# Summing weight blocks in the on-chip raw buffer instead of in HBM, in a hybrid conv and attention decoder

## The chip, the cores and the metric

The kernel runs on one core of a Trainium2 chip. The time is device microseconds of one execution of the whole program, the median of the runs that are shown. Beside it stands one execution recorded by the hardware profiler; its span goes from the first to the last instruction.

## The reference

The program is a decoder trunk of two layers on 512 tokens of width 1024, in float32. Layer 0 has a gated short convolution, layer 1 a sliding-window attention with sinks; each is followed by a SwiGLU feed-forward block of inner width 2816. Cut to what matters here:

```python
def swiglu(h, w_gate_up, w_down):
    g, u = jnp.split(h @ w_gate_up, 2, axis=-1)
    return (jax.nn.silu(g) * u) @ w_down

for l in range(DEPTH):                       # DEPTH = 2
    mix = short_conv_mixer(...) if l < N_A else sliding_window_sink_attention(...) @ b_w_o[j]
    h = h + rmsnorm(mix, ...)
    ff = swiglu(rmsnorm(h, ffn_pre_norm[l]), ffn_w_gate_up[l], ffn_w_down[l])
    h = h + rmsnorm(ff, ffn_post_norm[l])
```

## The kernel before, in words

**Products.** Every float32 matrix is split into a high and a low part of the fp32r type, and a product is three matmuls (hi by lo, hi by hi, lo by hi; `mm3`) or, in the gate stage, a wide matmul of the high weights with both parts of the tokens (L1088) and a narrow one of the low weights (L1091). The weights are split on the way: ScalarE copies a raw tile of 128x1024 into the high part (`whi`, L485), VectorE subtracts that from the raw tile for the low part (`wlo`, L486).

**Seven products for eight.** The gate and up columns are worked off in pairs, q = 0 to 9 in each layer (the names have the layer first: g05 is pair 5 of layer 0). A pair is a 2x2 scheme of blocks with seven products, numbered 1 to 7 and run in the order 1, 2, 6, 5, 7, 3, 4 (`gate_jobs`). Each needs a weight block or a sum of blocks. The sums s1 = a + b and s3 = a + c feed products 5 and 7. A third and a fourth sum feed products 6 and 3. For the pairs in `ADDED` (1, 2, 3, 4, 5, 7) these two are made on VectorE from tiles that are there anyway (`Job.add`, L473): product 6 reads a11 + s1 and product 3 reads a12 + (a11 + s1). For the other pairs they are made in HBM too. The down projection of a round (`down_jobs`) goes the same way with four sums in HBM.

**Sums in HBM.** `Sums` holds HBM tiles (`hsum`) and steps: copies of a block into them, then transfers that add another block, all issued on GpSimd's queue by `issue` (L554). The table `BEGIN` says at which stage each group of sums begins; `sum_on(stage)` issues what is left over, starts the new group, and takes one step of each open group. In the gate and down rounds `issue` is called after each job, for one transfer and a sixth of the backlog, each held back until ScalarE's `whi` of the job three ahead is made.

**The line of jobs.** `in_line` runs a layer's gate and down jobs, 106 of them, on TensorE in order. Three jobs ahead of the running one (`LINE_LEAD`), `prepare(j)` splits job j's weights; then it fetches by SP's queue (`Raw.fetch`, L456) each further raw tile whose buffer has been read for the last time, out of a ring of seven (`N_RAW`); then it makes the VectorE add for job j + 1. Raw tiles are fetched in the order of their first use. The pairs and rounds alternate: pairs 0 and 1, pair 2, down round 0, pair 3, pair 4, down round 1, pair 5, pair 6, down round 2, pair 7, pair 8, pair 9, down round 3. So the fetches for pairs 3, 5 and 7 are issued during a down round, those for pair 1 during pair 0.

**Evacuation.** VectorE and ScalarE take a product's PSUM banks into SBUF (L1043, L1066, L655) right behind it, in the same program order as the splits. The order of instructions on TensorE, VectorE, ScalarE and GpSimd is the order in which the code is written.

Of the kernel before, what the change touches and what calls it, by code (L numbers as in the profile page):

```python
# [13 lines left out]
ALU = mybir.AluOpType  # L14
# [4 lines left out]
S = 512  # L19
# [5 lines left out]
PLAIN = 2  # L25

ADDED = (1, 2, 3, 4, 5, 7)

BEGIN = {
# [52 lines left out]
def yoco_kernel(  # L82
# [22 lines left out]
    nc = tc.nc  # L105
# [15 lines left out]
    def name(s):  # L121
        uid[0] += 1
        return f"{s}_{uid[0]}"

    def slot(s, dt=F32, w=S):
        return big.tile([P, w], dt, tag="slot", name=name(s), padded_shape=[P, S])
# [37 lines left out]
    def fetch(src, n=D):  # L164
        raw = wraw.tile([P, D], F32, tag="raw", name=name("raw"))
        dst = raw[:, :n]
        if len(src.shape) == 3:
            src, dst = src.rearrange("k p c -> p k c"), dst.rearrange("p (k c) -> p k c", c=S)
        nc.sync.dma_start(dst, src)
        return raw  # L170

    class Two:


        def __init__(self, s, dt):
            self.of = [slot(s, dt) for _ in range(2)]
# [5 lines left out]
    def split_weights(src, raw=None, slots=False, eng=nc.vector):  # L182
        if raw is None:
            raw = fetch(src)
        if slots:
            hi, lo = Two("whi", F32R), Two("wlo", F32R)
            for h in range(2):
                c = slice(h * S, (h + 1) * S)
                nc.scalar.activation(hi[:, c], raw[:, c], AF.Copy)
                eng.tensor_tensor(out=lo[:, c], in0=raw[:, c], in1=hi[:, c].bitcast(F32),  # L190
                                  op=ALU.subtract)
            return hi, lo
        hi = wsp.tile([P, D], F32R, tag="whi", name=name("whi"))
        lo = wsp.tile([P, D], F32R, tag="wlo", name=name("wlo"))
        nc.scalar.activation(hi, raw, AF.Copy)
        nc.vector.tensor_tensor(out=lo, in0=raw, in1=hi.bitcast(F32), op=ALU.subtract)
        return hi, lo
# [45 lines left out]
    nc.sync.dma_start(xt[6], xT[6])  # L243
    nc.sync.dma_start(xt[7], xT[7])
    later = [fetch(w_in[1, t]) for t in range(min(3, N_RAW - 3))]


# [159 lines left out]
    class Ahead:  # L407
# [6 lines left out]
        def fetch(self, n):  # L414
            for _ in range(n):
                if self.srcs:
                    self.raws.append(fetch(self.srcs.pop(0)))
# [23 lines left out]
    class Raw:  # L441


        def __init__(self, *srcs):
            self.srcs = srcs
            self.widths = [s.shape[0] * S if len(s.shape) == 3 else D for s in srcs]
            self.n = sum(self.widths)

        def fetch(self):
            self.tile, c = wraw.tile([P, D], F32, tag="raw", name=name("raw")), 0  # L450
            for src, n in zip(self.srcs, self.widths):
                dst = self.tile[:, c : c + n]
                if len(src.shape) == 3:
                    src, dst = (src.rearrange("k p c -> p k c"),
                                dst.rearrange("p (k c) -> p k c", c=S))
                nc.sync.dma_start(dst, src)  # L456
                c += n

    class Job:

# [29 lines left out]
    def in_line(jobs, late, paced=True):  # L490

        raws = []
        for j, job in enumerate(jobs):
            for raw in job.raws:
                if raw not in raws:
                    raws.append(raw)
                raw.last = j
        n = [0]

        def prepare(j):  # L500

            if 0 <= j < len(jobs):
                jobs[j].prepare()
            while n[0] < len(raws) and (n[0] < N_RAW or raws[n[0] - N_RAW].last <= j):
                raws[n[0]].fetch()
                n[0] += 1
            if j + 1 < len(jobs):
                jobs[j + 1].add()

        for j in range(-1, LINE_LEAD):  # L510
            prepare(j)
        late = late()
        for j, job in enumerate(jobs):
            if job.run:
                job.run(job)
            prepare(j + LINE_LEAD)
            if paced and j + LINE_LEAD < len(jobs):
                issue(1 + len(issues) // 6, jobs[j + LINE_LEAD].begun)
            for _ in range(1 if paced else max(len(late) - 1, 1)):
                if late and not job.alone:  # L520
                    late.pop(0)()
            late += job.then() or [] if job.then else []
# [22 lines left out]
    def issue(n, behind=None):  # L545

        for dst, src, op in issues[:n]:
            if len(dst.shape) == 3:
                dst, src = (t.rearrange("k (a b) c -> (k a) (b c)", b=4) for t in (dst, src))
            else:  # L550
                dst, src = (t.rearrange("(a b) c -> a (b c)", b=2) for t in (dst, src))
            kw = {} if op is None else {"accum_op": op}
            made = tc.keep_in_program_order(
                nc.gpsimd.dma_start(dst, src, max_dma_last_dim=4 * 4 * S, **kw))  # L554
            if behind is not None:
                tc.add_manual_dep(
                    made.ins, behind.ins.name, mybir.DependencyInfo(
                        mybir.DependencyClass.Sync, mybir.DependencyReason.DATA),
                    reason="pace")
        del issues[:n]  # L560
# [3 lines left out]
    for l in range(2):  # L564
        for q in range((NF - PLAIN) // 2):
            sums_of[f"g{l}{q}"] = Sums([w_gb[l, q, b] for b in (2, 3, 0, 1)], [P, D],
                                        q not in ADDED)
        for rd, (f0, f1) in enumerate(ROUNDS[:-1]):
# [5 lines left out]
    def sum_on(at):  # L574

        issue(len(issues))
        if at in BEGIN:
            summing.append(sums_of[BEGIN[at]])
        for x in summing:
            x.step()  # L580
        summing[:] = [x for x in summing if x.steps]
# [88 lines left out]
    sums = small.tile([P, 4], F32, tag="sums", name=name("sums"))  # L670
# [6 lines left out]
    with tc.manual_schedule(engines=ALL):  # L677
# [25 lines left out]
        for k in range(KT):  # L703
# [7 lines left out]
            for i in range(3):  # L711
                for t in range(3):
                    n = 3 * k + t
# [117 lines left out]
    with tc.manual_schedule(engines=ALL):  # L831
        project(begun[1][2], ws[2], xs)

        def late():
            parts = []
            for f in range(2):
                first, second, taps, third, end = conv(f)
                first(begun[f][0])
                second(begun[f][1])
                parts += [taps, lambda third=third, f=f: third(begun[f][2])]  # L840
                sum_on(f"c{f}")
                issue(len(issues))
            return parts + end()
# [13 lines left out]
        for n in range(4):  # L857
            line[f"w{n}"] = closing = Job([Raw(w_out[n // 2, n % 2])], None)
            closing.slots = True
        in_line([line[n] for n in CONV.split()], late, False)  # L860
        ws = [line[f"w{n}"].w for n in range(4)]

# [109 lines left out]
    def first_weights(l):  # L972
        return ([w_gu[l, f, j] for f in range(2) for j in range(2)]
                + [w_gb[l, 0, b] for b in range(2)])

    sum_on("o0")
    issue(len(issues))
    ahead = Ahead(first_weights(0))
# [9 lines left out]
    def ffn(l, before, ahead, gain, gpres, following):  # L988
# [20 lines left out]
        def gate_jobs(q, factors, out, to, then):  # L1009
# [3 lines left out]
            sums = sums_of[f"g{l}{q}"]  # L1013
            a21, a22, a11, a12 = (Raw(b) for b in sums.blocks)
            s1, s3, *rest = (Raw(b) for b in sums.sums)
            raws = {1: [a11], 2: [a12], 5: [s1], 7: [s3], 4: [a22]}
            if rest:
                raws[6], raws[3] = ([r] for r in rest)
# [134 lines left out]
        with tc.manual_schedule(engines=ALL):  # L1153
# [30 lines left out]
            for rd, (f0, f1) in enumerate(ROUNDS):  # L1184
                last = rd == len(ROUNDS) - 1
                for f in range(max(f0, PLAIN), f1, 2):
                    q = (f - PLAIN) // 2
                    jobs += gate_jobs(q, factors, pair_acts if last else pair_sums, acts[rd],
                                      lambda q=q: sum_on(f"{l}p{q}"))
                    if behind_one and not (last and f < f1 - 2):  # L1190
                        jobs += behind_one.pop()
                if last:
                    break
                down = down_jobs(range(f0 // 2, f1 // 2), acts[rd], rd == 0,
                                 sums_of[f"d{l}{rd}"],
                                 lambda rd=rd: sum_on(f"{l}s{rd}"))
                behind_one.append(down)
            n = f1 - f0
# [6 lines left out]
            for at, job in zip(LAST, closing):  # L1205
                job.slots = True
                jobs.insert(len(jobs) - at, job)
            in_line(jobs, late)
            if l == 1:
                nc.gpsimd.drain()  # L1210
# [282 lines left out]
    at = []  # L1493
# [87 lines left out]
    with tc.manual_schedule(engines=ALL):  # L1581
        sum_on("a0")
        for i in range(KT + 2):
# [9 lines left out]
            for c in order.split():  # L1593
# [13 lines left out]
                op, n = c[0], [int(d) for d in c[1:].rstrip("-")]  # L1607
                t = i - late
                if op == "g":

                    u = 2 * (t - EARLY - 1) + n[0]
                    if u in (-2, -1, 2, 3):
                        j = u + 2 if u < 0 else u
# [123 lines left out]
```

## Time and profile before

| What | Value |
|---|---|
| median of 3 runs | 1015.68 us (1013.57 to 3697.7) |
| profiled execution | 1013.68 us |
| its span | 1011.9 us |
| busy: TensorE, VectorE, ScalarE, GpSimd | 99%, 88%, 58%, 20% |
| moved by DMA | 244.50 MB, mean 242 GB/s |
| transfers into hsum by GpSimd | 176 |

The page of the profile gives busy time by engine, the chain of work that ended last, groups of instructions by source line, and DMA issues with their time from issue to landing. A row of a group names line, engine, operation, output and inputs, shape and count, then busy time and the mean of one. A row of the timeline has start, length (of all instructions that it merges), engine, line and count. SPq and POOLq are the queues that issue transfers. A row of waits has the total, the count and the longest.

### The profile page before, as it was taken

To read this page: it belongs to the slowest core of one execution; us is meant where nothing else is said; L and a number is where in the kernel's file an instruction comes from. 1 tells how busy PE (TensorE), PEld (TensorE's weight loads), DVE (VectorE), ACT (ScalarE), POOL (GpSimd) and SP (SyncE) were. 2 spreads that over 40 slices of the span, in tenths; PEclk is the share of its full clock that TensorE was granted. 3 is DMA by queue.
4 is the path that set the end of the run, shared out by engine and by line. 5 is a ranking of instruction groups with operands and counts; after the bars stand their busy time and mean duration, and the time that the engine had idled before them with its cause. 6 is when DMAs were issued, how large, how long until landed. Compare 5 with 4: busy or idle time off the path is not lost.

```text
span 1011.9 us, 16084 instructions
## 1 busy us (share of the span) xinstructions
PE 1002.7 (99%) x5864; PEld 883.2 (87%) x5864; DVE 889.6 (88%) x1524; ACT 588.3 (58%) x1061; POOL 204.4 (20%) x265
## 2 busy tenths in 40 slices
PE   9999999999999999999999999999999999999997
PEld 8888888999889898898898887889998888989986
DVE  5766768899889999999888998988997999999996
ACT  6322544875656465566385788777666564645641
POOL 0443133102101011000022757331111010110001
PEclk9999999999999999999999999999999999999999
DMA  9997789549979789769603889985999576979742
GB/s 355 293 262 222 188 248 336 184 167 266 343 235 289 251 286 307 244 214 342 209 1 121 222 234 293 256 273 150 275 296 326 168 249 227 306 260 279 235 173 84
DMA packets 66575, 244.50 MB, mean 242 GB/s; under 512 B 7872, under 2 KB 8384, under 8 KB 54720
## 3 DMA queue, kind: packets, MB, share of 16 engines
q1 hardware_dynamic: 51328, 145.98, 38.8%
q0 software_dynamic: 14592, 96.48, 37.6%
q10 hardware_dynamic: 576, 1.02, 0.3%
q8 instruction: 46, 0.75, 0.3%
q14 instruction: 33, 0.27, 0.1%
HBM read 237.15 MB, written 102.76 MB: 336 GB/s over the span
## 4 chain that ended last, share of the span: by engine, by line
PE 96%; DVE 2%; ACT 1%; issue 0%; POOL 0%; DVEq 0%; POOLq 0%
PE gx L1088 15%; PE gx L1091 8%; PE pcub L200 4%; PE pcub L201 4%; PE pcub L202 4%; PE px L200 4%; PE px L201 4%; PE px L202 4%; PE pmix L202 3%; PE pmix L201 3%; PE pmix L200 3%; PE gz L1088 3%; PE gy L201 2%; PE gy L200 2%; PE gy L202 2%; PE pz L200 2%
## 5 line engine op out<-in xcount | busy, mean ns | idle before, releaser
L486 DVE TENSOR_TENSOR wlo<-raw,whi 128x1024 fp32r<-128x1024 f32 x225 | 274.7, 1225 | 33.5 <-ACT whi L485 33.4
L485 ACT ACTIVATE whi<-raw 128x1024 fp32r<-128x1024 f32 x225 | 233.7, 1051 | 99.1 <-DVE raw L473 28.7
L1088 PE MATMUL gx<-xt,whi 128*128 128x512 f32 x480 | 120.7, 393 | 0.0
L1088 PEld LDWEIGHTS gx<-xt,whi 128*128 128x128 f32 x480 | 86.2, 189 | 15.7
L554 POOL DMA_DIRECT2D hsum<-in_w_gb_dram x96 | 63.3, 745 | 146.1 <-ACT whi L485 89.0
L554 POOL DMA_DIRECT2D hsum<-hsum x32 | 25.3, 790 | 292.3 <-ACT whi L485 193.2
L1043 DVE TENSOR_TENSOR st<-gx,st 128x256 f32<-128x256 f32 x200 | 77.6, 419 | 2.2 <-ACT st L1066 0.4
L1066 ACT ACTIVATE st<-gx 128x256 f32<-128x256 f32 x120 | 43.5, 381 | 60.9 <-PE gx L1091 57.2
L1091 PEld LDWEIGHTS gx<-xt,wlo 128*128 128x128 f32 x480 | 65.5, 190 | 4.7
L1091 PE MATMUL gx<-xt,wlo 128*128 128x256 f32 x480 | 66.9, 282 | 0.0
L1102 ACT ACTIVATE gr<-gr 128x1024 f32<-128x1024 f32 x20 | 21.2, 1062 | 55.7 <-DVE gr L1043 55.7
L200 PE MATMUL px<-wlo,ahi 128*128 128x512 f32 x120 | 46.7, 389 | 0.0
L201 PE MATMUL px<-whi,ahi 128*128 128x512 f32 x120 | 46.7, 389 | 0.0
L202 PE MATMUL px<-whi,alo 128*128 128x512 f32 x120 | 46.7, 389 | 0.0
L200 PE MATMUL gy<-xlo,whi 128*128 128x256 f32 x160 | 45.3, 283 | 0.0
L201 PE MATMUL gy<-xhi,whi 128*128 128x256 f32 x160 | 45.3, 283 | 0.0
L202 PE MATMUL gy<-xhi,wlo 128*128 128x256 f32 x160 | 45.3, 283 | 0.0
L554 POOL DMA_DIRECT2D hsum<-in_w_dn_dram x48 | 32.4, 785 | 49.6 <-ACT whi L485 47.4
L1088 PE MATMUL gx<-xhl,whi 128*128 128x512 f32 x160 | 39.9, 391 | 0.0
L307 POOL TENSOR_TENSOR ur<-uv,mhalf 128x1 f32<-128x1 f32 x15 | 13.9, 925 | 121.8 <-DVE uv L303 121.7
L655 DVE TENSOR_TENSOR mix<-mix,px 128x512 f32<-128x512 f32 x54 | 34.9, 682 | 2.5 <-PE px L202 2.5
L473 DVE TENSOR_TENSOR raw<-raw,raw 128x1024 f32<-128x1024 f32 x28 | 34.1, 1219 | 0.0
(321 smaller groups left out, 3001.6 us busy)
## 6 DMA issues: line engine op xcount, KB each, us to landing
hsum<-in_w_gb_dram POOLq DMA_DIRECT2D x96, 512.0 KB, 7.7
raw<-hsum SPq DMA_DIRECT2D x88, 512.0 KB, 7.9
raw<-in_w_gb_dram SPq DMA_DIRECT2D x60, 512.0 KB, 6.6
hsum<-in_w_dn_dram POOLq DMA_DIRECT2D x36, 512.0 KB, 8.0
raw<-in_w_dn_dram SPq DMA_DIRECT2D x32, 512.0 KB, 6.7
hsum<-hsum POOLq DMA_DIRECT2D x28, 512.0 KB, 6.0
raw<-in_w_in_dram SPq DMA_DIRECT2D x21, 512.0 KB, 7.8
hsum<-in_w_dn_dram POOLq DMA_DIRECT2D x12, 768.0 KB, 12.0
```

The costliest lines, as they stand in the source:

```text
L200: nc.tensor.matmul(out, whi, xlo, start=start, stop=False, **kw)
L201: nc.tensor.matmul(out, whi, xhi, start=False, stop=False, **kw)
L202: nc.tensor.matmul(out, wlo, xhi, start=False, stop=stop, **kw)
L473: nc.vector.tensor_tensor(out=raw, in0=raw, in1=self.raws[1].tile, op=ALU.add)
L485: self.begun = nc.scalar.activation(hi[:, :n], raw, AF.Copy)
L486: nc.vector.tensor_tensor(out=lo[:, :n], in0=raw, in1=hi[:, :n].bitcast(F32), op=ALU.subtract)
L554: nc.gpsimd.dma_start(dst, src, max_dma_last_dim=4 * 4 * S, **kw))
L655: nc.vector.tensor_tensor(out=m, in0=m, in1=banks[bs][r], op=ALU.subtract if half else ALU.add)
L1043: nc.vector.tensor_tensor(out=out, in0=a, in1=b, op=ALU.add)
L1066: nc.scalar.activation(ste, a, AF.Copy)
L1088: nc.tensor.matmul(banks[c][e], whi[:, kk], factors[p][k][2], start=opened and k == 0, stop=False, **kw)
L1091: nc.tensor.matmul(banks[c][e][:, :256], wlo[:, kk], factors[p][k][0], start=False, stop=k == 3 and p in (4, 5), **kw)
```

## The change

For pairs 1, 3, 5 and 7 of each layer (`DIRECT`) the sums s1 and s3 are no longer made in HBM. Their raw tile is loaded by SP with the first block, and three `prepare` steps later GpSimd issues a transfer from HBM that adds the second block into the raw tile. `BEGIN`'s entries for these eight groups are passed over, so their copies and adds into HBM are not issued, and the transfers of other groups that stood behind them can be issued a stage or a job earlier.

```diff
+DIRECT = (1, 3, 5, 7)
...
     class Raw:
-        def __init__(self, *srcs):
-            self.srcs = srcs
+        def __init__(self, *srcs, plus=None):
+            self.srcs, self.plus = srcs, plus
...
+        def more(self):
+            tc.keep_in_program_order(nc.gpsimd.dma_start(
+                self.tile, self.plus, max_dma_last_dim=4 * 4 * S, accum_op=ALU.add))
...
         n = [0]
+        open_sums = []
         def prepare(j):
             if 0 <= j < len(jobs):
                 jobs[j].prepare()
             while n[0] < len(raws) and (n[0] < N_RAW or raws[n[0] - N_RAW].last <= j):
                 raws[n[0]].fetch()
+                if raws[n[0]].plus is not None:
+                    open_sums.append((j + 3, raws[n[0]]))
                 n[0] += 1
+            while open_sums and open_sums[0][0] <= j:
+                _, raw = open_sums.pop(0)
+                raw.more()
             if j + 1 < len(jobs):
                 jobs[j + 1].add()
...
         issue(len(issues))
-        if at in BEGIN:
+        if at in BEGIN and not (BEGIN[at][0] == "g" and int(BEGIN[at][2:]) in DIRECT):
             summing.append(sums_of[BEGIN[at]])
...
             s1, s3, *rest = (Raw(b) for b in sums.sums)
+            if q in DIRECT:
+                x, y, z, _ = sums.blocks
+                s1, s3 = Raw(x, plus=y), Raw(x, plus=z)
```

## The prediction, made before the changed kernel was run

> **What bounds the kernel now.** I read the page's head, then the chain, then TensorE's waits, and last the busy time of the gate and down stage, where the change lies.
>
> ```profile
> span 1011.9 us, 16084 instructions
> PE 1002.7 (99%) x5864; PEld 883.2 (87%) x5864; DVE 889.6 (88%) x1524; ACT 588.3 (58%) x1061; POOL 204.4 (20%) x265
> PE 96%; DVE 2%; ACT 1%; issue 0%; POOL 0%; DVEq 0%; POOLq 0%
> PE pt L1407 <- DVE s L1395: 1.2, 1, 1.2
> PE idle L683 <- DVE ones L149: 1.1, 1, 1.1
> 321.00:379.00 58.00, 58.00 (x340) 51.47 (x339) 57.02 (x88) 31.75 (x47) 7.53 (x12) 1.00 0.84 287
> 379.00:438.00 59.00, 59.00 (x345) 52.29 (x344) 57.51 (x89) 32.57 (x50) 6.73 (x10) 1.00 0.87 269
> ```
>
> TensorE is busy for 1002.7 of 1011.9 us, at a granted clock of 1.00 in both stretches, and the chain lies on it for 96%. It is seen to wait twice, 2.3 us together, for VectorE work in the attention layer and at the start, which the change does not touch. So no transfer that goes away can shorten the chain: it has nothing to give back. The two stretches of the first layer's rounds (start:end, length, then PE, PEld, DVE, ACT and POOL busy, clock, DMA share, GB/s) show the danger: VectorE is busy for 57.02 of 58 us. A wait put before VectorE there is made up again at about 1 us in 58 while TensorE runs on.
>
> **What is removed.** For each of eight pairs (1, 3, 5, 7 in two layers) two copies and two adding transfers into HBM go: 32 of GpSimd's 176 transfers.
>
> ```profile
> L554 POOL DMA_DIRECT2D hsum<-in_w_gb_dram x96 | 63.3, 745 | 146.1 <-ACT whi L485 89.0 <-ACT a L596 39.7 <-DMA hsum<-in_w_gb_dram 13.4
> L554 POOL DMA_DIRECT2D hsum<-hsum x32 | 25.3, 790 | 292.3 <-ACT whi L485 193.2 <-ACT a L596 89.3 <-issue 7.8
> hsum<-in_w_gb_dram POOLq DMA_DIRECT2D x96, 512.0 KB, 7.7
> raw<-hsum SPq DMA_DIRECT2D x88, 512.0 KB, 7.9
> raw<-in_w_gb_dram SPq DMA_DIRECT2D x60, 512.0 KB, 6.6
> hsum<-hsum POOLq DMA_DIRECT2D x28, 512.0 KB, 6.0
> ```
>
> That frees 32 x 745 ns = 23.8 us of GpSimd, which is busy 20%, and 16 MB of copies and adds out of 244.5 MB moved. Neither is on the chain: worth 0.
>
> **What is added and moved.** The 16 loads of a sum stay on SP in their places and only change their source (raw<-hsum, 7.9 us at the median, becomes raw<-in_w_gb_dram, 6.6). Sixteen adding transfers into the raw tile come on GpSimd, each about 790 ns of issue: 12.6 us, so GpSimd still saves some 11 us. The cost is not their issue but the series: SP's load must land, then GpSimd issues, then that lands, and only then may VectorE read the tile. The shortest time is that of s1 (the first sum), since product 6 of an ADDED pair needs a11 + s1 made on VectorE at L473. For layer 0 these are the issues of the s1 loads of pairs 1, 3, 5 and 7 (the first of each merged row), their landings (issues of the stretches 206:208, 276:277, 336:338 and 394:396, the last number us to landing), GpSimd's issue at the time of pair 1's, and the L473 rows that first read them.
>
> ```profile
> 206.94 4.22 SPq L456 DMA_DIRECT2D raw<-hsum  x2
> 276.07 1.46 SPq L456 DMA_DIRECT2D raw<-hsum  x2
> 336.04 2.66 SPq L456 DMA_DIRECT2D raw<-hsum  x2
> 394.36 2.66 SPq L456 DMA_DIRECT2D raw<-hsum  x2
> ...
> raw<-hsum SPq DMA_DIRECT2D x1, 512.0 KB, 3.2
> ...
> 211.10 0.53 POOL L554 DMA_DIRECT2D hsum<-in_w_gb_dram  x1 [0.49 <-ACT whi L485]
> ...
> raw<-hsum SPq DMA_DIRECT2D x1, 512.0 KB, 12.0
> ...
> raw<-hsum SPq DMA_DIRECT2D x1, 512.0 KB, 8.5
> hsum<-in_w_gb_dram POOLq DMA_DIRECT2D x1, 512.0 KB, 8.3
> ...
> raw<-hsum SPq DMA_DIRECT2D x1, 512.0 KB, 7.4
> ...
> 224.06 1.22 DVE L473 TENSOR_TENSOR raw<-raw,raw 128x1024 f32<-128x1024 f32 x1
> 291.90 1.22 DVE L473 TENSOR_TENSOR raw<-raw,raw 128x1024 f32<-128x1024 f32 x1
> 350.01 1.22 DVE L473 TENSOR_TENSOR raw<-raw,raw 128x1024 f32<-128x1024 f32 x1
> 408.51 1.22 DVE L473 TENSOR_TENSOR raw<-raw,raw 128x1024 f32<-128x1024 f32 x1
> ```
>
> Call A the time from the issue of the adding transfer to its landing. The trace has no adding transfer into SBUF. The nearest rows are adding transfers from HBM to HBM: hsum<-hsum, always an add, 6.0 us at the median, and the 8.3 us of the second one above. The worst company is in the convolution stage, 16.4 us for four at once (stretch 144:146):
>
> ```profile
> hsum<-in_w_gb_dram POOLq DMA_DIRECT2D x4, 512.0 KB, 16.4
> ```
>
> I take A = 6.5: the 6.0 of the same operation, and 0.5 for twice as many rows (128 of 4 KB for 64 of 8 KB). I keep 6.0 and 16.4 as ends. Lateness against the L473 row, with the load's landing at its place as it is now:
> - pair 1: landed at 206.94 + 3.2 = 210.1. The add comes three jobs after the load, behind GpSimd's issue at 211.10; landed by 218.1, with 6 us to spare.
> - pair 3: 276.07 + 12.0 + 6.5 = 294.6, 2.7 us after 291.90 (A - 3.8).
> - pair 5: 336.04 + 8.5 + 6.5 = 351.0, 1.0 late (A - 5.5).
> - pair 7: 394.36 + 7.4 + 6.5 = 408.3, 0.25 early (A - 6.75).
>
> Pair 3's 12.0 us are the longest because two copies for pair 7's sums are issued beside it; the change removes just these.
>
> ```profile
> 274.89 0.53 POOL L554 DMA_DIRECT2D hsum<-in_w_gb_dram  x1 [0.17 <-issue]
> 276.18 0.52 POOL L554 DMA_DIRECT2D hsum<-in_w_gb_dram  x1 [0.77 <-ACT whi L485]
> ...
> raw<-in_w_gb_dram SPq DMA_DIRECT2D x1, 512.0 KB, 6.4
> ```
>
> The last row is pair 5's next load from in_w_gb (stretch 340:342), 6.4 us. With such a load for the new source pairs 5 and 7 are 1.1 and 1.25 us early, so the lateness is 0 to 1 us there, and 0 to 2.7 at pair 3. In layer 1 the loads of pairs 3 and 5 take (stretches 771:772 and 831:832):
>
> ```profile
> raw<-hsum SPq DMA_DIRECT2D x1, 512.0 KB, 8.1
> ...
> raw<-hsum SPq DMA_DIRECT2D x1, 512.0 KB, 9.8
> ```
>
> So pair 3 would be early there and pair 5 1.3 us later than in layer 0, 2.3 in all. The second sum, s3, is read by ScalarE one or more products later and has 3 us more.
>
> **What hides it.** Behind a waiting L473 on VectorE stand the lo halves (L486) and the evacuations of products; ScalarE's whi of product 6 waits for it too. Pair 5's rows:
>
> ```profile
> 351.35 1.06 ACT L485 ACTIVATE whi<-raw 128x1024 fp32r<-128x1024 f32 x1 [4.73 <-DVE raw L473]
> 352.44 1.23 DVE L486 TENSOR_TENSOR wlo<-raw,whi 128x1024 fp32r<-128x1024 f32 x1
> 356.44 2.00 PE L1088 MATMUL gx<-xt,whi 128*128 128x512 f32 x8
> 360.98 1.22 DVE L486 TENSOR_TENSOR wlo<-raw,whi 128x1024 fp32r<-128x1024 f32 x1
> 364.82 0.28 PE L200 MATMUL gv<-xlo,whi 128*128 128x256 f32 x1
> ```
>
> Product 6's whi is ready at 352.41 and used at 356.44, 4.0 us later; product 3's lo is ready at 362.20 and its matmuls start at 364.82, 2.6 us later. So a lateness up to 2.6 us costs nothing; all above goes into the time one to one. Were this cover gone, 2.7 + 1.0 us in each of two layers would cost 7.4 us. GpSimd, too, now waits for the load before it issues, with the paced transfers of later sums behind it (pair 7: 397.25 on below). They move by some 5 us. Their sums are those of the last down round, and SP's first load of one is issued at 455.86.
>
> ```profile
> 397.25 0.52 POOL L554 DMA_DIRECT2D hsum<-in_w_dn_dram  x1 [2.15 <-ACT whi L485]
> ...
> 455.86 2.10 SPq L456 DMA_DIRECT2D raw<-hsum  x2
> ```
>
> The sum: 0 removed, 0 added. The profiled execution took 1013.68 us (span 1011.9 and 1.8 around it), so 1013.7. The median shown, 1015.68, is 2.0 above it, the lowest run 1013.57; I say 1014.
>
> The Trainium skill's page "DMA: Bandwidth & Descriptors", in "Anatomy of one DMA — SWDGE (gpsimd) path", fits 2.0 us plus bytes over 436 GB/s for such a transfer. By it A would be an estimated 3.2 us and every pair early; the 6.0 us row is nearly twice that, and I stay with the row.
>
> **Rivals.**
> - *The cover is too short.* If A is 8.3 to 10 us, the lateness is 4.5 to 6.2, 2.8 to 4.5 and 1.55 to 3.25 us at pairs 3, 5 and 7; less 2.6 each, 2.1 to 6.2 us per layer, 4 to 12 in all: 1018 to 1026. For it: the 8.3 row stands right there, with the DMA share at 0.84. Against it: that was the second of two back to back, and traffic falls. Chance 0.19.
> - *GpSimd's issue is held up by VectorE.* Were GpSimd kept from writing descriptors while VectorE runs, an issue would stretch by about two VectorE instructions of 1.22 us, so A = 9.0, and 2.6 + 0.9 us per layer over the cover: 1021. Against it: the 790 ns of the hsum<-hsum issues, made in stretches where VectorE is 98% busy, and the VectorE rows shown are all TENSOR_TENSOR. Chance 0.03. The Trainium skill's page "SBUF — State Buffer", section "SBUF: two separate sides", has this rule, for 2-port modes of VectorE alone.
> - *Slower by over 2%.* One mechanism: adding into SBUF takes so long that VectorE stalls at L473 in pairs 3, 5 and 7 of both layers. The cost per layer is 3A - 16.05 - 7.8; it reaches half of 20.3 us at A = 11.3. At 16.4 it would be some 51 us: 1064. Only the row of four at once speaks for it. Chance 0.05.
> - *Faster.* Even both of TensorE's waits away give 2.3 us: 1011.4. Over 2%: 0.01; a small gain: 0.01.
> - *It doesn't do what it says:* if the adds were held back so that the series became load, pause, add, that is the first rival's time.
>
> **How the numbers follow.** The forecast, 1012 to 1016.5, has 0.70. The range reaches into the first rival as far as A = 9.2 (3.9 us per layer, 1021.5), and up to 1022; below, to 1011.5, where TensorE's two waits are gone. 2% is what a measurement here can tell from no change; only the slow rival passes it, and what I have not thought of adds 0.01: faster 0.01, same 0.93, slower 0.06.
>
> **What would show it.** After: 32 fewer hsum transfers on POOL, 16 new ones raw<-in_w_gb_dram of about 0.8 us issue and 6 to 7 us landing; PE still 99% and without a new wait; among VectorE's waits a line raw L473 <- DMA raw of at most some 2 us each, for six times at most. Wrong would be: landings over 9 us, a PE wait on wlo L486 or whi L485 right behind an L473, or a span that moves by more than 8 us.

## The result and the profile after

The changed kernel takes 1021.59 us at the median (1019.8 to 1022.01), the kernel before 1014.74: ratio 1.0073, 95% interval 1.006 to 1.0085. One of the four runs of the kernel before took 3697.7 us and is in its median, but the ratio goes by the fast runs alone. By the ratio the changed kernel is slower by 7.4 us, clear of the spread. Its profiled execution took 1021.72 us; the span is 1020.0, 8.1 us longer than before.

From the page of the changed kernel: span, busy time, the chain by engine, the group of the VectorE add (L479 now, L473 before), and the issues of the loads and of the adding transfers (the last row is from the full list of issues).

```profile
span 1020.0 us, 16092 instructions
PE 1005.3 (99%) x5864; PEld 883.2 (87%) x5864; DVE 888.0 (87%) x1524; ACT 586.0 (57%) x1061; POOL 197.4 (19%) x249
PE 65%; DVE 20%; issue 7%; DMA 6%; ACT 1%; POOL 0%; DVEq 0%; SPq 0%; POOLq 0%; ACTq 0%
L479 DVE TENSOR_TENSOR raw<-raw,raw 128x1024 f32<-128x1024 f32 x28 | 34.2, 1220 | 16.7 <-DMA raw<-in_w_gb_dram 16.7
raw<-in_w_gb_dram SPq DMA_DIRECT2D x76, 512.0 KB, 6.6
hsum<-hsum POOLq DMA_DIRECT2D x28, 512.0 KB, 5.9
raw<-in_w_gb_dram POOLq DMA_DIRECT2D x16, 512.0 KB, 9.2
```

The busy share of TensorE is still 99% and hides the loss. The chain shows it: 96% on TensorE before, 65% now, with 20% on VectorE and 6% on transfers that no chain had before. VectorE's add waits 16.7 us for raw<-in_w_gb_dram, where it had waited for nothing. The adding transfer takes 9.2 us to its landing at the median of all sixteen, the HBM add hsum<-hsum still 5.9.

The waits (total, times, longest) of TensorE and of VectorE's add:

```profile
PE gx L1103 <- DVE st L1058: 6.2, 9, 1.6
DVE raw L479 <- DMA raw<-in_w_gb_dram: 16.7, 5, 4.1
```

Pair 5 of layer 0 in the changed kernel, from the timelines of SP, GpSimd, VectorE, ScalarE and TensorE (start, length, what ended the idle time before):

```profile
335.94 9.65 SPq L458 DMA_DIRECT2D raw<-in_w_gb_dram  x5
345.30 0.86 POOL L462 DMA_DIRECT2D raw<-in_w_gb_dram  x1 [8.52 <-DMA raw<-in_w_gb_dram]
346.48 0.86 POOL L462 DMA_DIRECT2D raw<-in_w_gb_dram  x1 [0.32 <-DVE mix L667]
353.55 1.22 DVE L479 TENSOR_TENSOR raw<-raw,raw 128x1024 f32<-128x1024 f32 x1 [3.54 <-DMA raw<-in_w_gb_dram]
354.88 1.06 ACT L491 ACTIVATE whi<-raw 128x1024 fp32r<-128x1024 f32 x1 [8.36 <-DVE raw L479]
355.98 1.23 DVE L492 TENSOR_TENSOR wlo<-raw,whi 128x1024 fp32r<-128x1024 f32 x1
357.12 0.75 DVE L1058 TENSOR_TENSOR st<-gx,st 128x256 f32<-128x256 f32 x2
357.59 0.73 PE L1103 MATMUL gx<-xt,whi 128*128 128x512 f32 x2 [1.09 <-DVE st L1058]
```

The load of s1 is issued at 335.94 as foreseen. The add follows at 345.30 and lands in time for VectorE to go on at 353.55; it would have been there at 350.01. Behind it stand the split and then the evacuation of product 1, st at 357.12; TensorE's product 6 starts at 357.59 when the first half of st is done. Product 6's high part had been ready at 355.94, its low part at 357.21: not its weights but the bank that it adds into came last.

The other three large waits, in the same views:

```profile
414.27 1.22 DVE L479 TENSOR_TENSOR raw<-raw,raw 128x1024 f32<-128x1024 f32 x1 [3.76 <-DMA raw<-in_w_gb_dram]
418.32 0.50 PE L1103 MATMUL gx<-xt,whi 128*128 128x512 f32 x1 [1.31 <-DVE st L1058]
852.83 1.23 DVE L479 TENSOR_TENSOR raw<-raw,raw 128x1024 f32<-128x1024 f32 x1 [4.07 <-DMA raw<-in_w_gb_dram]
856.88 0.50 PE L1103 MATMUL gx<-xt,whi 128*128 128x512 f32 x1 [1.62 <-DVE st L1058]
913.41 1.23 DVE L479 TENSOR_TENSOR raw<-raw,raw 128x1024 f32<-128x1024 f32 x1 [3.62 <-DMA raw<-in_w_gb_dram]
917.46 0.50 PE L1103 MATMUL gx<-xt,whi 128*128 128x512 f32 x1 [1.17 <-DVE st L1058]
```

In all four the wait less TensorE's idle time is 2.45 us (3.54 - 1.09, 3.76 - 1.31, 4.07 - 1.62, 3.62 - 1.17). That is the cover at the start of product 6. These four make 5.2 us of TensorE's 6.2.

They are not the whole price. TensorE runs the same 5864 matmuls in the same order in both traces; set side by side, they show where the changed kernel falls behind. In each of these four pairs it loses 0.9 us more than the idle time above: the first matmuls of product 6 and of product 7 follow each other more slowly, and product 4 waits for st again:

```profile
369.54 2.09 PE L1103 MATMUL gx<-xt,whi 128*128 128x512 f32 x8 [0.20 <-DVE st L1058]
```

The four pairs lose 1.98, 2.20, 2.51 and 2.07 us, each its wait less 1.56 us. So the cover of the pair as a whole is 1.56 us, and what passes that is paid one to one: 8.8 us in all. Small losses elsewhere in these rounds add 0.8, and 1.1 us come back in the attention layer and 0.4 at the start, which makes the 8.1 us of the span.

### The profile page after: what moved, and what is told of

It is laid out like the page before. It is cut to its first block, busy times and chain, and to the rows that moved or that the text cites. A ratio compares the mean times of both kernels' runs of the same rounds, so it can differ in the third digit from the quotient of the medians.

```text
span 1020.0 us, 16092 instructions
## 1 busy us (share of the span) xinstructions
PE 1005.3 (99%) x5864; PEld 883.2 (87%) x5864; DVE 888.0 (87%) x1524; ACT 586.0 (57%) x1061; POOL 197.4 (19%) x249
## 4 chain that ended last, share of the span: by engine, by line
PE 65%; DVE 20%; issue 7%; DMA 6%; ACT 1%; POOL 0%; DVEq 0%; SPq 0%; POOLq 0%; ACTq 0%
PE gx L1103 7%; DVE wlo L492 6%; DMA raw<-in_w_gb_dram 5%; DVE st L1058 4%; PE pcub L204 4%; PE pcub L203 4%; PE pcub L202 4%; PE gx L1106 4%; PE pmix L204 3%; PE pmix L203 3%; PE pmix L202 3%; DVE alo L619 2%; PE pcub L727 2%; PE px L203 2%; PE px L202 2%
## 5 line engine op out<-in xcount | busy, mean ns | idle before, releaser
L566 POOL DMA_DIRECT2D hsum<-in_w_gb_dram x64 | 41.3, 678 | 126.0 <-ACT whi L491 56.8
L479 DVE TENSOR_TENSOR raw<-raw,raw 128x1024 f32<-128x1024 f32 x28 | 34.2, 1220 | 16.7 <-DMA raw<-in_w_gb_dram 16.7
```

Source lines behind the costliest of these rows:

```text
L479: nc.vector.tensor_tensor(out=raw, in0=raw, in1=self.raws[1].tile, op=ALU.add)
```

## The experiments

The theory to be tested, L: the time is lost where VectorE waits at the add of a11 + s1, for what the wait exceeds the cover. Its rival Q: GpSimd's queue, which now waits for SP's loads with other transfers behind it, or the moved transfers.

**Only s3 by adding transfer.** s1 is made in HBM as before.

```diff
+            if q in DIRECT:
+                made = sums_of[f"g{l}{q}"]
+                made.steps = [[x for x in step if x[0] is made.sums[0]] for step in made.steps]
...
-        if at in BEGIN and not (BEGIN[at][0] == "g" and int(BEGIN[at][2:]) in DIRECT):
+        if at in BEGIN:
...
-                s1, s3 = Raw(x, plus=y), Raw(x, plus=z)
+                s3 = Raw(x, plus=z)
```

> Pairs 1, 3, 5 and 7 make only the second sum s3 by load and adding transfer; s1 is made in HBM as before. Theory L (the time is lost where VectorE waits at the add of a11 + s1 in pairs 3, 5 and 7, for the part of the wait above about 1.8 us): no wait of VectorE on a raw tile, ratio to before 1.000 +- 0.0015. Rival Q (GpSimd's queue, which now waits for SP's loads with the paced transfers behind it, or the moved transfers, cost the time): the eight adding transfers still wait for loads, so about half of the 7 us stays, ratio 1.003 to 1.004.

Measured: 0.9993 (0.9984 to 1.0002). VectorE has no wait on a raw tile and TensorE none on st, though eight adds still make GpSimd wait. L holds.

**Only s1 by adding transfer**, to learn whether the neighbouring add of s3 makes that of s1 late. The steps kept in HBM are here those of `made.sums[1]`.

```diff
...
-                s1, s3 = Raw(x, plus=y), Raw(x, plus=z)
+                s1 = Raw(x, plus=y)
```

> Pairs 1, 3, 5 and 7 make only the first sum s1 by load and adding transfer; s3 is made in HBM as before. Theory C (an adding transfer lands late because that of s3, issued 1.2 us behind it on the same queue, shares the 16 engines with it): the time from issue to landing falls from 7.4 to 8.9 us in pairs 5 and 7 to about 6 to 6.5, the waits at the add from 3.6 to 4.1 us to 1 to 2, at or under the cover of 1.8; ratio 1.000 to 1.002. Rival I (it is the adding transfer itself that takes so long): landing after 8 to 9 us as before, waits of 3.5 to 4 us, ratio 1.007.

Measured: 1.007 (1.0056 to 1.0084), the whole loss with half the adds. Waits of VectorE and issues:

```profile
DVE raw L479 <- DMA raw<-in_w_gb_dram: 16.6, 6, 4.3
raw<-in_w_gb_dram POOLq DMA_DIRECT2D x8, 512.0 KB, 8.6
```

Theory C falls: the eight adds of s1 landed after 8.6 us at the median in the changed kernel too, and the wait is nearly the same, 16.6 us for 16.7.

**s1 fetched first.** All adds stay; s1's load takes its place in the ring ahead of a11 and a12.

```diff
...
-            for raw in job.raws:
+            for raw in (*job.early, *job.raws):
                 if raw not in raws:
                     raws.append(raw)
-                raw.last = j
+            for raw in job.raws:
+                raw.last = j
...
+            if q in DIRECT:
+                made[0].early = (s1,)
```

> All adding transfers stay; in these pairs the load of s1 is fetched ahead of those of a11 and a12, two places earlier in the ring of raw tiles. Theory L: the series load, add, VectorE starts two jobs (about 5 us) earlier, so that every s1 has landed before VectorE comes to it: no wait on a raw tile, ratio 1.000 +- 0.0015, with 8 MB less moved than before. Rival Q: the same transfers and the same waits of GpSimd, ratio 1.006 to 1.007.

Measured: 0.9989 (0.998 to 0.9998). There is no wait on a raw tile; the adds of

```profile
raw<-in_w_gb_dram POOLq DMA_DIRECT2D x16, 512.0 KB, 7.4
```

land in time. The same transfers two fetches earlier cost nothing, so neither their number nor GpSimd's queue is the cause. Run a second time:

> The kernel with s1 fetched ahead of a11 and a12, once more, to see whether it is faster than the kernel before by more than the spread. If the 8 MB less are worth something, 0.998 to 0.9995 again; if TensorE alone sets the time, 1.000 +- 0.001.

Measured: 0.9991 (0.9982 to 1.0). Against the kernel before, both point 1 us down, at the edge of what can be told. The traces say where such a microsecond lies: TensorE's wait for s in the attention layer is 0.2 us in both, 1.2 before (see the next section). That the 8 MB less are worth anything is not shown. This is the version to keep: as fast as the kernel before or 0.1% faster, with 8 MB less moved.

**Single pairs.** First `DIRECT = (1,)`:

> Only pair 1 of each layer makes its two sums by load and adding transfer. Theory L: pair 1's s1 landed 2.8 to 3.7 us ahead of VectorE in the changed kernel, so this costs nothing: ratio 1.000 +- 0.0015. Rival Q, by which each such pair costs alike: a quarter of the 7.3 us, ratio 1.0018.

Measured: 1.002 (1.0011 to 1.0029), the number that Q had given, and a miss of mine. The trace, however, has a wait at the add in one layer. Waits, and the issues of stretch 707:708.5:

```profile
DVE raw L479 <- DMA raw<-in_w_gb_dram: 1.5, 1, 1.5
PE gx L1103 <- DVE st L1058: 1.2, 1, 1.2
...
hsum<-in_w_gb_dram POOLq DMA_DIRECT2D x2, 512.0 KB, 10.0
raw<-in_w_gb_dram POOLq DMA_DIRECT2D x1, 512.0 KB, 13.7
```

With the sums of pairs 3, 5 and 7 back in HBM, three transfers into hsum are issued within 2 us ahead of pair 1's add in layer 1, and it lands after 13.7 us, not the 9.5 of the changed kernel. I read from this that what was safe there is late here by the queue's company. The wait of 1.5 us costs TensorE all of its 1.5 us: pair 1 has no cover to speak of, and why it lacks the 1.56 us of pairs 5 and 7 was not looked into. So L holds in kind, but not with one cover for all pairs. Then `DIRECT = (5,)`:

> Only pair 5 of each layer makes its two sums by load and adding transfer. Theory L (each wait at the add costs what is above 1.8 us): waits of 3.5 to 4.1 us in each layer, 3.4 to 4.6 us in all, ratio 1.0035 to 1.0045. Rival Q (each such pair costs alike): a quarter of the whole, ratio 1.0018.

Measured: 1.0057 (1.0043 to 1.0071), three times Q's number.

```profile
DVE raw L479 <- DMA raw<-in_w_gb_dram: 6.8, 2, 3.5
PE gx L1103 <- DVE st L1058: 2.3, 4, 1.1
```

The waits are those foreseen. Less 1.56 us each they make 3.7, and the profiled execution, 1017.56 us, is 4.1 above the kernel before, as L has it; the other runs reach 1020.5, and why they are up to 3 us longer is not settled.

**The add one job later** on VectorE, in pairs 3, 5 and 7.

```diff
+                if jobs[j].late_add:
+                    jobs[j].add()
                 jobs[j].prepare()
...
-            if j + 1 < len(jobs):
+            if j + 1 < len(jobs) and not jobs[j + 1].late_add:
                 jobs[j + 1].add()
...
+            made[2].late_add = q in DIRECT and q > 1
```

> The changed kernel with its transfers; in pairs 3, 5 and 7 VectorE's add of a11 + s1 stands one job later in its order, behind the evacuation of product 1 (st) and not ahead of it. Theory E (TensorE waits because the evacuation stands behind the waiting add, with 1.8 us of cover): VectorE comes to the add some 2.8 us later, its wait falls from 3.6 to 4.1 us to about 1, TensorE no longer waits for st, and product 6's high part (4.0 us of cover) is just in time: ratio 1.000 to 1.002. Rival W (TensorE waits for product 6's own weights, which the late sum makes late): the sum lands when it did and the split follows as late or later, ratio 1.007 or more.

Measured: 1.0066 (1.0053 to 1.0079). Waits, then VectorE's rows of pair 5:

```profile
DVE raw L479 <- DMA raw<-in_w_gb_dram: 8.8, 5, 2.5
PE gx L1105 <- DVE st L1060: 5.6, 7, 1.6
...
355.02 1.22 DVE L479 TENSOR_TENSOR raw<-raw,raw 128x1024 f32<-128x1024 f32 x1 [2.37 <-DMA raw<-in_w_gb_dram]
357.45 1.23 DVE L492 TENSOR_TENSOR wlo<-raw,whi 128x1024 fp32r<-128x1024 f32 x1 [1.21 <-ACT whi L491]
358.59 0.74 DVE L1060 TENSOR_TENSOR st<-gx,st 128x256 f32<-128x256 f32 x2
```

The wait at the add halves, but st still stands behind add and split, and now the split waits 1.21 us for ScalarE as well. My edit did not do what its text says, so the time does not tell E from W. The next one puts the split off too, in the same three pairs.

```diff
...
+            if 0 < j < len(jobs) and jobs[j - 1].put_off:
+                jobs[j - 1].add()
+                jobs[j - 1].prepare()
-            if 0 <= j < len(jobs):
+            if 0 <= j < len(jobs) and not jobs[j].put_off:
                 jobs[j].prepare()
...
-            if j + 1 < len(jobs):
+            if j + 1 < len(jobs) and not jobs[j + 1].put_off:
                 jobs[j + 1].add()
...
+            made[2].put_off = q in DIRECT and q > 1
```

> The changed kernel with its transfers; in pairs 3, 5 and 7 both the add of a11 + s1 and product 6's split stand one job later, so that now the evacuation of product 1 (st) is ahead of them on VectorE and ScalarE. (The edit before this one had moved the add behind the down product's evacuation only, and st stayed behind it.) Theory E (TensorE waits for st, which stands behind the waiting add): TensorE's wait for st goes; the sum has landed when VectorE comes to it; product 6's high part is ready 0 to 0.5 us after TensorE wants it; ratio 1.000 to 1.003. Rival W (TensorE waits for product 6's own weights, which the late sum makes late): the weights are ready as late as in the changed kernel or later, ratio 1.007 or more.

Measured: 1.0106 (1.0092 to 1.012), slower still. TensorE's waits, and VectorE at pair 5:

```profile
PE gx L1106 <- DVE st L1061: 4.3, 8, 0.9
PE gx L1106 <- ACT whi L491: 2.0, 6, 0.3
...
354.38 0.91 DVE L1061 TENSOR_TENSOR st<-gx,st 128x256 f32<-128x256 f32 x2 [2.01 <-ACT st L1084]
355.20 1.22 DVE L479 TENSOR_TENSOR raw<-raw,raw 128x1024 f32<-128x1024 f32 x1
357.60 2.36 DVE L492 TENSOR_TENSOR wlo<-raw,whi 128x1024 fp32r<-128x1024 f32 x2 [1.18 <-ACT whi L491]
```

The time alone is W's number, but the waits are E's: VectorE waits for no raw tile, and TensorE's wait at product 6 is 0.3 us on whi. The new order leaves VectorE idle for 2.01 + 1.18 us itself, and later products wait for st, up to 0.9 us. So idle time of VectorE is paid for here though no transfer ends it, and the ratio that I expected left that out.

**Why the add takes long.** The kernel before with its gate sums in HBM written as 128 rows of 4 KB:

```diff
-                dst, src = (t.rearrange("(a b) c -> a (b c)", b=2) for t in (dst, src))
+                dst, src = (t[:, :] for t in (dst, src))
```

> The kernel before, with its gate sums in HBM moved as 128 rows of 4 KB in place of 64 of 8 KB. If twice as many rows make an adding transfer slow, hsum<-hsum takes over 7.5 us to its landing at the median (6.0 before); if it is the company of the transfer, 6 to 6.5. The time stays within 0.2% in both cases, since those sums are made long before they are read.

Measured: ratio 1.0008 (0.9998 to 1.0018). The landing of hsum<-hsum, and the packets of this run; the second line is, figure for figure, that of the kernel before:

```profile
hsum<-hsum POOLq DMA_DIRECT2D x28, 512.0 KB, 6.5
DMA packets 66575, 244.50 MB, mean 242 GB/s; under 512 B 7872, under 2 KB 8384, under 8 KB 54720
```

So the edit changed the rows in the program and not on the chip: the sums still move in packets of 8 KB, and the run says nothing about rows. Nor are the 0.5 us over the 6.0 of before an effect: the same row reads 5.5 to 6.2 in the runs that leave these adds as they were. Then the changed kernel with `accum_op` left out of its sixteen transfers:

> The changed kernel with its adding transfers turned into plain copies into the same raw tiles at the same places; the addition is left out, so the sums are not formed. Theory R (reading, adding and writing back is what makes the transfer long): a copy of the same bytes lands in about 5.5 to 6 us in pairs 3, 5 and 7 (6.9 to 9.1 for the adds), VectorE's waits at the add fall by about 2.5 us each to 1 to 1.5, under the cover of 2.3 in pairs 5 and 7: ratio 1.000 to 1.001. Rival K (company: SP's loads in flight at the same time, and the time until GpSimd's first packet): the copy lands after 7 to 9 us too, waits near 3.5 us, ratio 1.005 to 1.007.

Measured: 1.001 (1.0001 to 1.0019).

```profile
raw<-in_w_gb_dram POOLq DMA_DIRECT2D x16, 512.0 KB, 6.3
DVE raw L479 <- DMA raw<-in_w_gb_dram: 4.5, 2, 2.3
PE gx L1103 <- DVE st L1058: 0.4, 2, 0.2
```

A copy in the same place lands 2.9 us sooner at the median of all sixteen. For the six sums s1 of pairs 3, 5 and 7, on which the loss rests, the median falls from 7.8 us (6.9 to 9.1) to 5.4 (5.0 to 6.8). Two waits of at most 2.3 us are left, and nearly all of the loss is gone; product 6 starts in time, and each of the two pairs still loses the 0.7 us by which its wait passes 1.56. GpSimd waits for the loads as before: Q falls here too, and K with its 7 to 9 us for the copy. The adding makes up 2.4 of the 7.8 us by these medians, and without it the loss is gone.

## Why the prediction was wrong

The range held the time, and the first rival, "the cover is too short", had the mechanism, a late add, with 1018 to 1026 us. The forecast, no change, was wrong. Of the three signs of being wrong two came, landings over 9 us (9.2) and a span that moved by more than 8 us (8.1); TensorE's wait came too, but for st and not for a weight.

- *TensorE bounds the kernel and nothing is to be gained:* nearly right. But the change does touch one of the two waits that I had set aside, that in the attention layer. GpSimd's and VectorE's rows there, before and after, and TensorE's wait after:

```profile
625.62 1.29 POOL L554 DMA_DIRECT2D hsum<-in_w_gb_dram  x2
626.70 2.77 POOL L190 TENSOR_TENSOR wlo<-raw,whi 128x512 fp32r<-128x512 f32 x2
626.75 2.74 DVE L1390 TENSOR_TENSOR se<-se,rs 128x4 f32<-128x4 f32 x1
...
629.42 0.77 POOL L566 DMA_DIRECT2D hsum<-hsum  x1
629.98 2.77 POOL L192 TENSOR_TENSOR wlo<-raw,whi 128x512 fp32r<-128x512 f32 x2
631.08 1.70 DVE L1405 TENSOR_TENSOR se<-se,rs 128x4 f32<-128x4 f32 x1
PE pt L1422 <- DVE s L1410: 0.2, 1, 0.2
```

  VectorE's small operation, 0.16 us long elsewhere, ends in both with GpSimd's (629.49 and 629.47, 632.78 and 632.75), and s follows it. With two issues fewer ahead of it GpSimd is done earlier, and TensorE waits 0.2 us, not 1.2. With one fewer (only s3, only s1) the wait is 0.7 and 0.8, with none fewer (single pairs) 1.3 and 1.2. So what the change removes was worth 1 us, where I had 0; that GpSimd holds VectorE up is read from these rows.
- *A, the step that failed.* I took 6.5 us and so found pairs 5 and 7 of layer 0 late by 1 us at most. The series of load, issue and add of the six sums s1, in us:

| Pair, layer | load, foreseen | measured | landing to issue | A, foreseen | measured | late, foreseen | wait at the add |
|---|---|---|---|---|---|---|---|
| 3, 0 | 12.0 | 10.1 | 0.6 | 6.5 | 6.9 | 2.7 | 1.7 |
| 5, 0 | 8.5 | 8.7 | 0.6 | 6.5 | 8.2 | 1.0 | 3.5 |
| 7, 0 | 7.4 | 9.8 | 0.5 | 6.5 | 7.4 | -0.25 | 3.8 |
| 3, 1 | 8.1 | 5.2 | 0.7 | 6.5 | 7.3 | early | none |
| 5, 1 | 9.8 | 8.5 | 0.6 | 6.5 | 8.9 | 2.3 | 4.1 |
| 7, 1 | - | 7.9 | 0.6 | 6.5 | 9.1 | - | 3.6 |

- A was too small in all six, by 0.4 to 2.6 us. My 6.0 came from adding transfers as well, so the adding alone is not what I missed; the place is. Two stretches, that of an hsum<-hsum that lands after 5.1 us before, and that of pair 5's add after (the last numbers are clock, DMA share and GB/s):

```profile
355.40:360.50 5.10, 5.10 (x33) 4.55 (x32) 5.07 (x8) 2.40 (x4) 1.28 (x2) 1.00 0.73 157
345.30:353.50 8.20, 8.20 (x42) 6.96 (x41) 4.70 (x6) 1.06 (x1) 1.72 (x2) 1.00 1.04 274
```

  The DMA engines are full while pair 5's add is under way. That this is why it lands later is my reading; no run varied SP's loads alone. Of my 0.5 us for twice as many rows no run shows anything.
- I had the 8.3 row at the same place and set it aside for a median over calmer places. At A = 8.3 my own formula gives 4.2 us, at 9.2 7.8 us; 7.4 were measured. That the last two are close is luck: the formula takes 5.6 of the 7.8 from pair 3, which cost 0.4 us, where pairs 5 and 7 cost 8.8. The 8.3 row, too, is close to pair 5's 8.2 in part by luck: it was the second of two, and the first landed after 5.9, while the add of s1 is the first of its two.
- *The load:* I hoped for 6.4 us from the new source in pairs 5 and 7. It was 8.7 in pair 5 of layer 0 (stretch 335:336), as long as from hsum (8.5), and in pair 7 of layer 0 it is the term that I had most wrong, 9.8 for 7.4. Pair 3's still took 10.1 us with the two copies gone that I had called the reason for its 12.0. And some 0.6 us between the load's landing and the add's issue (344.7 and 345.30 in pair 5) was not in the sum.
- *Pair 5 summed anew:* 335.94 + 8.7 + 0.6 + 8.2 = 353.5, 3.5 late as measured, where I had 1.0 (8.2 is the landing at 353.5 less the issue). The add's transfer gives 1.7 of the difference.
- *The cover:* 2.6 foreseen, 2.45 measured at product 6 in pairs 5 and 7, so the size was nearly right there, but for the wrong reason. I looked at when product 6 and 3 need their weights; what came first was the bank that product 6 adds into, read out by st behind the add. And the pair as a whole has 1.56, pair 3 1.24 (1.68 us of wait, 0.44 lost), pair 1 none.
- *GpSimd's saving, its delayed sums, s3:* right in that no wait on the chain names the last two. GpSimd's busy time fell by 7 us (11 foreseen).
- *GpSimd's issue held up by VectorE:* no. The issue took 0.86 us in the rows above.
- *The fit that would have every pair early.* The fit in the Trainium skill's page "DMA: Bandwidth & Descriptors" ("Anatomy of one DMA — SWDGE (gpsimd) path"), an estimated 3.2 us, is half of the 6.3 us that even the plain copies took in this traffic.

## What to carry to other kernels

A load that is followed by an adding transfer is a series, and its price is not the number of transfers but the time at which the last lands against the in-order engine that reads it; started two fetches earlier, it cost nothing here. Where an engine is busy for 98%, ask of any wait that you put on it what stands behind it in program order, the freeing of banks above all, and not only who needs its result. Take the duration of a new transfer from a row at the same place and in the same company, not from a median over the program, and look at the DMA share there. And when an edit is to change the shape of a transfer, look at the packets in the trace to see that it did.

## What the runs showed of the hardware

An adding transfer into the raw tile costs about twice the engine time of a copy. In the records of single packets, those of 4 KB on GpSimd's queue took 349 ns on average in the changed kernel (2048 of them) and 171 ns with `accum_op` left out, SP's plain ones 175 ns. The 8 KB packets of the sums in HBM, half of them adds, gather around 309 and 629 ns in the kernel before. For the six sums s1 of pairs 3, 5 and 7 the first packet started 2.6 us after the issue and the packets took 4.2 us from first to last, at the median; with `accum_op` left out it was 2.4 and 2.3 us. So the adding lengthens the packets' part and hardly the time before it. How much of the rest comes from transfers ahead on the same queue and how much from SP's loads was not taken apart.
